# RWKV products in unbroken bursts over four quadrants, an output bank opened by its first product, and adaLN weights loaded at high priority

## The chip, the core and the metric

The kernel runs on one core of a Trainium2 chip, with its five engines: TensorE (PE in the profile; its weight loads are PEld), VectorE (DVE), ScalarE (ACT), GpSimd (POOL) and SyncE (SP), which here issues most DMAs. The metric is the device time of one execution in microseconds.

## What is computed

Two layers of a hybrid backbone over 512 latent and 256 context tokens of width 1024. Layer 0 mixes with a bidirectional RWKV-7 (12 heads of 64) and a pooling mixer, then a SwiGLU FFN; layer 1 is a neighbourhood attention and an FFN. Every sub-layer is modulated by adaLN vectors: `mod = silu(c) @ ada_w[i] + ada_b[i]`. The change lies in the RWKV recurrence and in the adaLN products:

```python
def wkv_scan(S0, r, w, k, v, kk, b, reverse):
    def step(S, inp):
        r_t, w_t, k_t, v_t, kk_t, b_t = inp
        sa = -jnp.einsum('bhij,bhj->bhi', S, kk_t)
        S = S * w_t[:, :, None, :] + sa[..., :, None] * b_t[:, :, None, :] + v_t[..., :, None] * k_t[:, :, None, :]
        return S, jnp.einsum('bhij,bhj->bhi', S, r_t)
    ...
for d in range(2):
    S_c, yc = wkv_scan(S0, ...context..., rev)
    _, yl = wkv_scan(S_c, ...latents..., rev)
```

## The kernel before

**GEMMs.** Activations lie transposed, features on partitions. Each f32 GEMM is made of three f32r products of split operands (hi x hi, lo x hi, hi x lo): lines L123 to L125, in `mm3`. Their banks are named g (layer 0's input projections), s (the context's output projection and FFN, 256 columns) and y or w (the latents, 512 columns). `mm3` keeps its last product in `self.last`.

**RWKV.** The recurrence is worked out in chunks of 64 tokens. A `Job` takes two head pairs (`pair`, `pair + 1`; l in the code), both directions (d), and four chunks; there are nine, three for the context and six for the latents. In each, the two heads (h) of a pair lie on partitions 0 to 63 and 64 to 127 (`hd[h]`). A job has
- `prep`: `scores` (L1157, 16 products of 64 x 64 by 128 columns for each l and d, so 36 groups of 16) and `tokens` transposes, for both l and d; then `inverse`, the inverse of a triangular 64 x 64 matrix for each chunk, whose 16 x 16 diagonal blocks DVE works out (L1191, L1192; the blocks go to it through HBM, tensors ar, L, td) and whose larger blocks TensorE joins in the steps s1 to s5;
- `chain`: four steps, one after the other. A step makes g (L1285), the first part of the output y (L1293, in a bank that two zero products of L1291 opened, since several products add up in it), copies the state into the next one's bank (L1298), then pa (L1302), the new rows of ST (ACT copies for head 0, DVE for head 1), the new state pS (L1315), which DVE scales into the next ST, and the last part of y (L1328).

The array of TensorE is 128 x 128. A product with 64 rows and 64 columns takes a quadrant of it. In what follows A and D are the two on the diagonal (rows and columns 0 to 63, rows and columns 64 to 127), B and C the other two (B: rows 0 to 63, columns 64 to 127). An f32 product appears in the profile as two records.

**Order.** The code gives each instruction a priority: `level(n)` sets the class (0 is served first) and within it the order of writing counts. A list scheduler with a timeline of its own then writes each engine's queue; an engine works its queue off in order. `issue_after(x)` forces an instruction behind x on the queue of the same engine, and lets others stand between. `emit` deals out several generators by their costs: in the latents' RWKV part a job's `chain` is level 0, the next job's `prep` level 2, and the context's output projection and FFN (s) level 8, which fills TensorE.

**adaLN.** `adas` multiplies silu(c) with `ada_w`: eight products of 32 output columns for a group of 512 features, in two bursts of four, one for each column strip (L201), then four small ones (L213) that turn the result. The weights come by `ada_loads` (SP, L180). In layer 0's mix groups 4 to 11 run at level 5, and their loads land in the three `wraw` buffers that the input weights `w_in` (L115) use too. Layer 1's twelve groups run at level 9, dealt out beside the latents' first FFN, with four buffers `aw` of their own.

## Time and profile before

| | |
|---|---|
| median of 3 runs (lowest, highest) | 2385.91 us (2370.8, 2388.42) |
| the profiled execution | 2381.51 us, its span 2379.5 us |
| busy: PE, PEld | 2163.1 us (91%), 1735.9 us (73%) |
| busy: DVE, ACT, POOL | 1226.7 us (52%), 994.5 us (42%), 660.5 us (28%) |
| granted TensorE clock, mean | 0.937 of 2.4 GHz |

Busy times are unions of an engine's instructions; a TensorE that is busy need not be at its peak. Up to about 690 us the input projections and the context's RWKV run, up to about 1015 us the latents' RWKV with the context's GEMMs as filler; then the context's rest and the latents' output projection and FFN, and from about 1620 us layer 1.

### The profile page before, as it was taken

To read this page: it belongs to the slowest core of one execution; us is meant where nothing else is said; L and a number is where in the kernel's file an instruction comes from. 1 tells how busy PE (TensorE), PEld (TensorE's weight loads), DVE (VectorE), ACT (ScalarE), POOL (GpSimd) and SP (SyncE) were. 2 spreads that over 40 slices of the span, in tenths; PEclk is the share of its full clock that TensorE was granted. 3 is DMA by queue.
4 is the path that set the end of the run, shared out by engine and by line. 5 is a ranking of instruction groups with operands and counts; after the bars stand their busy time and mean duration, and the time that the engine had idled before them with its cause. 6 is when DMAs were issued, how large, how long until landed. Compare 5 with 4: busy or idle time off the path is not lost.

```text
span 2379.5 us, 44426 instructions
## 1 busy us (share of the span) xinstructions
PE 2163.1 (91%) x16944; PEld 1735.9 (73%) x16944; DVE 1226.7 (52%) x2529; ACT 994.5 (42%) x2075; POOL 660.5 (28%) x643
## 2 busy tenths in 40 slices
PE   6787988889879898979999999998999998999995
PEld 4676666556657777757788887787878876888874
DVE  2666555636746764244534453347556665333343
ACT  3545344444534544334443342224455644322332
POOL 2442213121322433456642310005224442000021
PEclk9889999879879899999999999999999998999997
DMA  7766476666753544576544335332432112333331
GB/s 262 224 187 188 121 205 186 175 176 187 228 142 89 137 128 112 169 233 214 162 150 118 116 120 167 113 91 88 133 105 63 51 63 66 97 92 100 96 90 63
DMA packets 324677, 327.34 MB, mean 138 GB/s; under 512 B 137328, under 2 KB 214768, under 8 KB 324464
## 3 DMA queue, kind: packets, MB, share of 16 engines
q1 hardware_dynamic: 320720, 317.45, 45.1%
q10 hardware_dynamic: 2592, 3.90, 0.5%
q8 instruction: 133, 2.18, 0.4%
q0 software_dynamic: 1152, 3.15, 0.3%
q14 instruction: 80, 0.66, 0.1%
HBM read 280.02 MB, written 42.80 MB: 136 GB/s over the span
## 4 chain that ended last, share of the span: by engine, by line
PE 62%; DVE 6%; DMA 5%; issue 2%; ACT 2%; SPq 1%; POOL 1%; POOLq 0%; ACTq 0%; DVEq 0%
PE y L123 7%; PE y L125 7%; PE y L124 7%; PE w L123 6%; PE w L124 6%; PE w L125 6%; PE s L123 3%; PE s L125 3%; PE s L124 3%; PE s L743 1%; PE w L1157 1%; DMA wraw<-w 1%; PE v L201 1%; PE v L725 1%; PE y L700 1%
## 5 line engine op out<-in xcount | busy, mean ns | idle before, releaser
L887 ACT CAST whi<-wraw 128x512 fp32r<-128x512 f32 (+2 forms) x560 | 330.2, 594 | 674.1 <-PE y L124 261.0
L888 DVE TENSOR_TENSOR wlo<-wraw,whi 128x512 fp32r<-128x512 f32 (+2 forms) x384 | 293.1, 767 | 339.6 <-ACT whi L887 316.1
L888 POOL TENSOR_TENSOR wlo<-wraw,whi 128x512 fp32r<-128x512 f32 (+2 forms) x176 | 202.3, 1155 | 299.4 <-ACT whi L887 270.7
L123 PE MATMUL w<-lhhi,whi 128*128 128x512 f32 x472 | 189.3, 403 | 11.3 <-ACT lhhi L1012 5.8
L110 POOL TENSOR_TENSOR wlo<-wraw,whi 128x512 fp32r<-128x512 f32 x92 | 121.4, 1323 | 280.1 <-ACT whi L109 233.3
L123 PE MATMUL y<-lhhi,whi 128*128 128x512 f32 x488 | 192.3, 394 | 0.5 <-ACT lhhi L752 0.5
L124 PE MATMUL y<-lhlo,whi 128*128 128x512 f32 x488 | 190.7, 391 | 0.0
L125 PE MATMUL y<-lhhi,wlo 128*128 128x512 f32 x488 | 190.6, 391 | 0.0
L124 PE MATMUL w<-lhlo,whi 128*128 128x512 f32 x472 | 186.4, 395 | 1.3 <-DVE lhlo L937 1.1
L125 PE MATMUL w<-lhhi,wlo 128*128 128x512 f32 x472 | 185.6, 393 | 0.1
L913 POOL TENSOR_TENSOR lxz<-lxz,s 128x512 f32<-128x512 f32 x28 | 43.3, 1578 | 508.9 <-ACT s L919 508.9
L123 PE MATMUL s<-chhi,whi 128*128 128x256 f32 x480 | 145.5, 303 | 19.6 <-DVE kclo L616 7.8
L123 PE MATMUL g<-hhi,whi 128*128 128x256 f32 (+1 forms) x368 | 139.1, 378 | 17.4 <-DVE nr L486 4.5
L125 PE MATMUL s<-chhi,wlo 128*128 128x256 f32 x480 | 143.2, 298 | 1.1 <-POOL wlo L888 1.1
L124 PE MATMUL s<-chlo,whi 128*128 128x256 f32 x480 | 143.3, 299 | 0.4 <-DVE chlo L937 0.4
L125 PE MATMUL g<-hhi,wlo 128*128 128x256 f32 (+1 forms) x368 | 135.6, 369 | 2.2 <-POOL wlo L110 2.1
L124 PE MATMUL g<-hlo,whi 128*128 128x256 f32 (+1 forms) x368 | 132.6, 360 | 0.0
L123 PEld LDWEIGHTS s<-chhi,whi 128*128 128x128 f32 x480 | 97.2, 203 | 29.9 <-ACT whi L887 8.8
L123 PEld LDWEIGHTS w<-lhhi,whi 128*128 128x128 f32 x472 | 89.2, 190 | 36.0 <-ACT lhhi L984 7.4
L123 PEld LDWEIGHTS y<-lhhi,whi 128*128 128x128 f32 x488 | 92.1, 189 | 22.1 <-issue 3.0
L124 PEld LDWEIGHTS w<-lhlo,whi 128*128 128x128 f32 x472 | 89.3, 189 | 23.6 <-DVE lhlo L937 4.2
L125 PEld LDWEIGHTS y<-lhhi,wlo 128*128 128x128 f32 x488 | 91.9, 188 | 19.8 <-DVE n L937 0.8
(376 smaller groups left out, 5048.3 us busy)
## 6 DMA issues: line engine op xcount, KB each, us to landing
wraw<-w SPq DMA_DIRECT2D x368, 256.0 KB, 2.6
aw<-ada_w SPq DMA_DIRECT2D x128, 256.0 KB, 4.7
wraw<-w_in SPq DMA_DIRECT2D x92, 256.0 KB, 3.3
bk<-bk SPq DMA_DIRECT2D x72, 256.0 KB, 4.3
wraw<-ada_w SPq DMA_DIRECT2D x64, 256.0 KB, 3.4
wraw<-w_out SPq DMA_DIRECT2D x48, 256.0 KB, 3.0
wraw<-wk SPq DMA_DIRECT2D x32, 256.0 KB, 2.9
wraw<-wv SPq DMA_DIRECT2D x32, 256.0 KB, 3.1
```

Of the source, the lines that this page charges most:

```text
L110: (self.nc.gpsimd if POOL_LO else self.nc.vector).tensor_tensor(out=lo, in0=raw, in1=hi, op=ALU.subtract)
L123: mm(ps, lhsT=lh, rhs=rh, start=first, stop=False)
L124: mm(ps, lhsT=lh, rhs=rl, start=False, stop=False)
L125: self.last = mm(ps, lhsT=ll, rhs=rh, start=False, stop=last)
L201: mm = nc.tensor.matmul(ps[32 * q:32 * q + 32, part], lhsT=self.cs[:, k + q, :], rhs=w[q // step][:, q % step, :], start=k == 0, stop=k > ...
L700: return lambda: mm(banks[j][:, 256 * c:256 * c + 256], lhsT=q[i == 2][hd, cb * P:cb * P + P], rhs=r[i == 1][hd, cs], start=i == 0, stop=i ...
L725: turn = lambda j, i: lambda: nc.tensor.transpose(out=pt[j][:, i, :], in_=s[j][:, i * P:i * P + P], identity=self.ident)
L743: return lambda: mm(po[64 * j:64 * j + 64, :], lhsT=src[:, hc], rhs=sT[j][:, i, :], start=i == 0, stop=i == 3)
L887: self.nc.scalar.copy(out=hi, in_=raw)
L888: self.lo.tensor_tensor(out=lo, in0=raw, in1=hi, op=ALU.subtract)
L913: tt = lambda o, x, y, op, e=V: e.tensor_tensor(out=o, in0=x, in1=y, op=op)
L1157: nc.tensor.matmul(ps[w][hd[h ^ w], c, :], lhsT=bk[hd[h], w, c, :], rhs=LH[0][hd[h], c, :], start=True, stop=True,)
```

## The change

- `burst(calls)` is new: each product is issued after the one ahead of it.
- Scores: one burst of 16 that goes c outside, then w = 1, 0, then h, where w was outside. By quadrants: B C A D, four times, where it was A D four times and then B C four times.
- s1 to s5 and all products of a chain step become bursts, with head 1 ahead of head 0. pS goes by turns between the heads; before it did the four of head 0 and then the four of head 1.
- The zero products (L1291) go. The output bank is opened by the first product of each head (`start=l == d == 0`).
- `ada_loads` issues its DMAs at level 0, whatever the level of the products.
- The four adaLN products of a burst are issued after each other, the first of them after `self.last`, the last GEMM product written so far.

```diff
@@ ada_loads, adas
-                    self.nc.sync.dma_start(out=wv, in_=src[:, k:k + step, part])
+                    with self.level(0):
+                        self.nc.sync.dma_start(out=wv, in_=src[:, k:k + step, part])
...
-                    first = None
-                    for q in (3, 2, 1, 0):
-                        with self.tc.issue_after(first.ins) if first else nullcontext():
-                            mm = nc.tensor.matmul(
...
-                        first = first or mm
+                    with self.tc.issue_after(self.last.ins) if self.last else nullcontext():
+                        self.burst([lambda q=q: nc.tensor.matmul(
+                            ps[32 * q:32 * q + 32, part], lhsT=self.cs[:, k + q, :], rhs=w[q // step][:, q % step, :],
+                            start=k == 0, stop=k > 0, tile_position=(0, 32 * q)) for q in (3, 2, 1, 0)])
@@ burst
+    def burst(self, calls):
+        last = None
+        for c in calls:
+            with self.tc.issue_after(last.ins) if last else nullcontext():
+                last = c()
@@ scores
-        for w in range(2):
-            for c in range(4):
-                for h in range(2):
-                    nc.tensor.matmul(
-                        ps[w][hd[h ^ w], c, :], lhsT=bk[hd[h], w, c, :], rhs=LH[0][hd[h], c, :],
-                        start=True, stop=True,
-                    )
+        K.burst([
+            lambda w=w, c=c, h=h: nc.tensor.matmul(
+                ps[w][hd[h ^ w], c, :], lhsT=bk[hd[h], w, c, :], rhs=LH[0][hd[h], c, :], start=True, stop=True,
+            ) for c in range(4) for w in (1, 0) for h in range(2)
+        ])
@@ inverse, and so s2 to s5
-        uh = [(u, h) for u in range(8) for h in range(2)]
+        uh = [(u, h) for u in range(8) for h in (1, 0)]
-            for u, h in uh:
-                mm(px[hd[h], u, :], lhsT=A1[g][hd[h], u, :], rhs=Tm[g][hd[h], u, :], start=True, stop=True)
+            K.burst([lambda u=u, h=h: mm(
+                px[hd[h], u, :], lhsT=A1[g][hd[h], u, :], rhs=Tm[g][hd[h], u, :], start=True, stop=True) for u, h in uh])
@@ chain, and so pg, pa and the last py
-        ldh = [(l, d, h) for l in range(2) for d in range(2) for h in range(2)]
+        ldh = [(l, d, h) for l in range(2) for d in range(2) for h in (1, 0)]
-            for h in range(2):
-                mm(flat(py[hd[h]]), lhsT=K.zero[hd[h], 0:64], rhs=K.zero[hd[h], 0:256], start=True, stop=False)
-            for l, d, h in ldh:
-                mm(py[hd[h], d, l, :], lhsT=LH[l][d][h][:, ci[d], 64:128], rhs=ST[h][:, l, si, d, :], start=False, stop=False)
+            K.burst([lambda l=l, d=d, h=h: mm(
+                py[hd[h], d, l, :], lhsT=LH[l][d][h][:, ci[d], 64:128], rhs=ST[h][:, l, si, d, :],
+                start=l == d == 0, stop=False) for l, d, h in ldh])
...
-                for h in range(2):
-                    m0 = None
-                    for l in range(2):
-                        for d in range(2):
-                            with K.tc.issue_after(m0.ins) if m0 else nullcontext():
-                                m0 = mm(pS[hd[h], l, d, :], lhsT=TOK[l][d][:, h, ci[d], :], rhs=ST[h][:, l, si, d, :],
-                                        start=s == 0, stop=s == 0 or l == d == 1)
+                K.burst([lambda l=l, d=d, h=h: mm(
+                    pS[hd[h], l, d, :], lhsT=TOK[l][d][:, h, ci[d], :], rhs=ST[h][:, l, si, d, :],
+                    start=s == 0, stop=s == 0 or l == d == 1) for l, d, h in ldh])
```

Since the scheduler sees other instructions and constraints, all queues are written anew. At three places TensorE's queue reads as follows (tile names carry their buffer numbers).

The first score group of the first job, before: w_1338 is the bank of w = 0 (quadrants A and D), w_1339 that of w = 1 (B and C); L424 and L456 are products of `keys`, L496 a transpose.

```order
L424 MATMUL k_1040<-lora_511,lw_953 128x256
L496 MATMUL g_924<-cst_63,sq_808 128x128 x2
L1157 MATMUL w_1338<-lh_1331,bk_1328 64x128 x8
L1157 MATMUL w_1339<-lh_1331,bk_1328 64x128 x8
L456 MATMUL k_1132<-lora_552,lw_953 128x256
L123 MATMUL g_949<-hhi_427,whi_939 128x256
```

The same group after the change:

```order
L421 MATMUL k_1040<-lora_511,lw_953 128x256
L493 MATMUL g_924<-cst_63,sq_808 128x128 x2
L1160 MATMUL w_1339<-lh_1331,bk_1328 64x128 x2
L1160 MATMUL w_1338<-lh_1331,bk_1328 64x128 x2
L1160 MATMUL w_1339<-lh_1331,bk_1328 64x128 x2
L1160 MATMUL w_1338<-lh_1331,bk_1328 64x128 x2
L1160 MATMUL w_1339<-lh_1331,bk_1328 64x128 x2
L1160 MATMUL w_1338<-lh_1331,bk_1328 64x128 x2
L1160 MATMUL w_1339<-lh_1331,bk_1328 64x128 x2
L1160 MATMUL w_1338<-lh_1331,bk_1328 64x128 x2
L453 MATMUL k_1132<-lora_552,lw_953 128x256
L123 MATMUL g_949<-hhi_427,whi_939 128x256
```

The two banks now take turns, two products each; nothing else is changed around them.

The first chain step of the last job, before (c is the bank of g, S of the state, y of the output; L1298 copies the state):

```order
L1285 MATMUL c_13834<-ST_13027,lh_13279 64x64
L1285 MATMUL c_13834<-ST_13028,lh_13280 64x64
L1298 MATMUL S_13856<-ST_13027,cst_63 64x256
L1298 MATMUL S_13856<-ST_13028,cst_63 64x256
L1291 LDWEIGHTS zero_67
L1291 MATMUL y_13845<-zero_67 64x256
L1291 LDWEIGHTS zero_67
L1291 MATMUL y_13845<-zero_67 64x256
L1293 MATMUL y_13845<-ST_13027,lh_13087 64x64
L1293 MATMUL y_13845<-ST_13028,lh_13088 64x64
L1293 MATMUL y_13845<-ST_13027,lh_13135 64x64
```

The same step after the change:

```order
L1287 MATMUL c_13770<-ST_12969,lh_13151 64x64
L1287 MATMUL c_13770<-ST_12970,lh_13222 64x64
L1287 MATMUL c_13770<-ST_12969,lh_13221 64x64
L1293 MATMUL y_13781<-ST_12970,lh_13030 64x64
L1293 MATMUL y_13781<-ST_12969,lh_13029 64x64
L1293 MATMUL y_13781<-ST_12970,lh_13078 64x64
L1293 MATMUL y_13781<-ST_12969,lh_13077 64x64
L1293 MATMUL y_13781<-ST_12970,lh_13152 64x64
```

The zero products with their weight loads are gone, the heads have changed places (ST_12970 is head 1), and the output's first burst follows that of g at once; the state's copy (L1300) comes behind it. In one other step of this job GEMM products of the context stand between the two bursts.

The adaLN products of layer 1's second group, before, in the RWKV chain of the last job (v is their bank):

```order
L125 MATMUL s_6938<-chhi_6885,wlo_8165 128x256
L123 MATMUL s_6938<-chhi_6885,whi_8182 128x256
L124 MATMUL s_6938<-chlo_6886,whi_8182 128x256
L201 MATMUL v_14894<-aw_14883,cs_69 32x512
L1315 MATMUL S_13968<-ST_13027,tok_13122 64x64
L1315 MATMUL S_13968<-ST_13027,tok_13168 64x64
```

The first burst of layer 1's first group, after the change:

```order
L125 MATMUL s_6914<-g_8945,wlo_9139 128x256
L124 MATMUL w_14627<-lhlo_14131,whi_14630 128x512
L125 MATMUL w_14627<-lhhi_14130,wlo_14631 128x512
L200 MATMUL v_14646<-aw_14644,cs_69 32x512
L200 MATMUL v_14646<-aw_14642,cs_69 32x512
L200 MATMUL v_14646<-aw_14640,cs_69 32x512
L200 MATMUL v_14646<-aw_14638,cs_69 32x512
L124 MATMUL y_14628<-lhlo_14131,whi_14687 128x512
L125 MATMUL y_14628<-lhhi_14130,wlo_14688 128x512
```

It has moved from the last RWKV jobs to the latents' FFN (y, w, 512 columns): of layer 1's 96 products 48 stood ahead of the context's 1200th GEMM product, and now none does. On SP the loads of `w_in` and `ada_w` into the three `wraw` buffers keep their sequence among each other; ada loads stand up to some eight places further ahead among the other DMAs.

## Rows read from the trace of the kernel before

**Rows 1.** Windows of three stages: busy us (and count) by engine; granted clock, DMA share, GB/s.
```profile
0.00:690.00 690.00, 572.09 (x5751) 428.54 (x5751) 398.12 (x988) 305.99 (x725) 177.74 (x169) 0.89 0.66 193
690.00:1015.00 325.00, 296.27 (x4202) 247.70 (x4203) 174.61 (x475) 145.68 (x337) 118.72 (x122) 0.89 0.47 126
...
1110.00:1620.00 510.00, 506.91 (x2617) 417.87 (x2616) 233.35 (x356) 188.70 (x343) 133.35 (x118) 1.00 0.41 127
```

**Rows 2.** The chain that ended last, by line, in 525:690, 690:1015 and 1015:1110 us.
```profile
by line: PE g L123 6.6%; PE g L125 5.7%; PE g L124 5.5%; PE w L1157 5.4%; DMA kk<-kk 4.8%; issue 4.0%; DMA wraw<-w_out 3.5%; DMA mt<-mix 3.5%; DMA wraw<-ada_w 2.6%; PE g L565 2.4%; SPq L870 2.4%; DMA gate<-gate 2.4%; DMA kk<-k 2.4%; DMA bk<
...
by line: PE s L123 7.7%; PE s L124 6.8%; PE s L125 6.8%; PE w L1157 6.0%; DVE pr L1191 5.6%; PE S L1315 4.1%; issue 3.7%; PE c L1302 3.7%; PE c L1285 3.3%; DMA wraw<-w 3.3%; PE y L1328 3.1%; DMA ar<-AR 2.8%; DMA L<-ar 2.7%; PE y L1293 2.7%;
...
by line: DMA wraw<-w 13.3%; PE s L123 9.4%; PE s L125 9.1%; PE s L124 8.0%; PE v L201 8.0%; DMA lxz<-xp 6.0%; POOL wlo L888 5.9%; DMA aw<-ada_w 5.4%; POOL lxz L871 3.3%; PE w L124 3.2%; issue 3.0%; PE w L125 2.9%; PE w L123 2.9%; DVE Y L136
```

**Rows 3.** Groups of PE in 690:1015 (two) and in 525:690 us (one).
```profile
L1157 PE MATMUL w<-lh,bk 64*64 64x128 f32 x384 | 27.7, 304 | 0.7 <-PE y L1328 0.6
L1315 PE MATMUL S<-ST,tok 128*64 128x64 f32 x272 | 19.8, 233 | 0.7 <-DVE ST L1305 0.7
...
L1157 PE MATMUL w<-lh,bk 64*64 64x128 f32 x256 | 18.0, 285 | 0.9 <-DVE lh L1109 0.9
```

**Rows 4.** Timeline of PE: start, duration (us), line, operation, records; three places.
```profile
532.05 1.09 PE L1157 MATMUL w<-lh,bk 64*64 64x128 f32 x16
533.07 0.97 PE L1315 MATMUL S<-ST,tok 128*64 128x64 f32 x16
...
756.60 1.59 PE L1157 MATMUL w<-lh,bk 64*64 64x128 f32 x32 [0.65 <-PE y L1328]
758.12 0.87 PE L1285 MATMUL c<-ST,lh 128*64 128x64 f32 x16
...
902.22 0.63 PE L1302 MATMUL c<-g,TT 64*64 64x64 f32 x16
902.68 1.32 PE L1157 MATMUL w<-lh,bk 64*64 64x128 f32 x28
```

**Rows 5.** Timeline of PE in 975:981 us, a chain step between GEMMs.
```profile
975.41 0.28 PE L123 MATMUL s<-chhi,whi 128*128 128x256 f32 x1
975.53 0.28 PE L124 MATMUL s<-chlo,whi 128*128 128x256 f32 x1
975.74 0.97 PE L1315 MATMUL S<-ST,tok 128*64 128x64 f32 x16
976.63 0.68 PE L1328 MATMUL y<-ST,RB 64*64 64x64 f32 x16
...
979.62 0.69 PE L1285 MATMUL c<-ST,lh 128*64 128x64 f32 x16
980.23 0.30 PE L1291 MATMUL y<-zero 64*64 64x256 bf16 x2
980.46 0.69 PE L1293 MATMUL y<-ST,lh 128*64 128x64 f32 x16
```

**Rows 6.** Groups of PE over the whole span: busy, mean ns, idle before, releasers.
```profile
L1157 PE MATMUL w<-lh,bk 64*64 64x128 f32 x1152 | 81.0, 303 | 11.8 <-DVE lh L1109 10.4 <-ACT tok L1141 0.7 <-PE y L1328 0.6
...
L1315 PE MATMUL S<-ST,tok 128*64 128x64 f32 x528 | 39.7, 235 | 2.6 <-ACT ST L1304 1.9 <-DVE ST L1305 0.7
```

**Rows 7.** Waits of PE and of SP's DMA queue: total us, times, longest.
```profile
PE g L201 <- DMA wraw<-ada_w: 20.1, 11, 3.4
...
SPq L180 <- PE g L201: 17.5, 13, 4.7
```

**Rows 8.** Groups of PE in 960:1110 us: the adaLN products of layer 1.
```profile
L201 PE MATMUL v<-aw,cs 128*32 128x512 f32 x96 | 18.3, 710 | 2.5 <-DMA aw<-ada_w 2.5
...
L213 PE MATMUL v<-cst,md 128*128 128x2 f32 x40 | 4.9, 241 | 0.7 <-ACT md L210 0.7
```

**Rows 9.** Windows of the two long stretches at half clock.
```profile
460.00:494.00 34.00, 24.79 (x140) 14.66 (x142) 18.35 (x64) 12.60 (x34) 0.00 (x0) 0.50 0.70 194
679.00:706.00 27.00, 19.05 (x208) 15.61 (x209) 16.39 (x41) 10.91 (x25) 11.52 (x13) 0.50 0.55 133
```

More of the change, by code (lines that the diff above doesn't have):

```diff
@@ L77, in __init__ @@
         self.now = 0
-        self.tail = None
+        self.tail = self.last = None
         self.ps = {}
@@ L196, in adas @@
                     w = [ready.pop(0) for _ in range(count)]
-                    first = None
-                    for q in (3, 2, 1, 0):
-                        with self.tc.issue_after(first.ins) if first else nullcontext():
-                            mm = nc.tensor.matmul(
-                                ps[32 * q:32 * q + 32, part], lhsT=self.cs[:, k + q, :], rhs=w[q // step][:, q % step, :],
-                                start=k == 0, stop=k > 0, tile_position=(0, 32 * q),
-                            )
-                        first = first or mm
+                    with self.tc.issue_after(self.last.ins) if self.last else nullcontext():
+                        self.burst([lambda q=q: nc.tensor.matmul(
+                            ps[32 * q:32 * q + 32, part], lhsT=self.cs[:, k + q, :], rhs=w[q // step][:, q % step, :],
+                            start=k == 0, stop=k > 0, tile_position=(0, 32 * q)) for q in (3, 2, 1, 0)])
                     if k == 0 or part.stop < 512:
@@ L1242, in s2 @@
             p1 = K.bank(self.v, (8, 32))
-            for u, h in uh:
-                mm(p1[lo[h], u, :], lhsT=TT[g][lo[h], u, 0:32], rhs=X1[g][lo[h], u, 0:32], start=True, stop=True,
-                   tile_position=(64 * h, 64 * h))
+            K.burst([lambda u=u, h=h: mm(
+                p1[lo[h], u, :], lhsT=TT[g][lo[h], u, 0:32], rhs=X1[g][lo[h], u, 0:32], start=True, stop=True,
+                tile_position=(64 * h, 64 * h)) for u, h in uh])
             for h in range(2):
@@ L1249, in s3 @@
             p2 = K.bank(self.v, (8, 64))
-            for u, h in uh:
-                mm(p2[hd[h], u, :], lhsT=X1[g][hd[h], u, :], rhs=TT[g][hd[h], u, :], start=True, stop=True)
+            K.burst([lambda u=u, h=h: mm(
+                p2[hd[h], u, :], lhsT=X1[g][hd[h], u, :], rhs=TT[g][hd[h], u, :], start=True, stop=True) for u, h in uh])
             V.tensor_tensor(out=TT[g], in0=TT[g], in1=p2, op=ALU.subtract)
@@ L1255, in s4 @@
             p3 = K.bank(self.v, (8, 32))
-            for u, h in uh:
-                mm(p3[up[h], u, :], lhsT=A1[g][lo[h], u, 32:64], rhs=Tm[g][lo[h], u, 0:32], start=True, stop=True,
-                   tile_position=(64 * h, 64 * h + 32))
+            K.burst([lambda u=u, h=h: mm(
+                p3[up[h], u, :], lhsT=A1[g][lo[h], u, 32:64], rhs=Tm[g][lo[h], u, 0:32], start=True, stop=True,
+                tile_position=(64 * h, 64 * h + 32)) for u, h in uh])
             for h in range(2):
@@ L1262, in s5 @@
             p4 = K.bank(self.v, (8, 32))
-            for u, h in uh:
-                mm(p4[lo[h], u, :], lhsT=Tm[g][up[h], u, 0:32], rhs=TT[g][up[h], u, 32:64], start=True, stop=True,
-                   tile_position=(64 * h + 32, 64 * h))
+            K.burst([lambda u=u, h=h: mm(
+                p4[lo[h], u, :], lhsT=Tm[g][up[h], u, 0:32], rhs=TT[g][up[h], u, 32:64], start=True, stop=True,
+                tile_position=(64 * h + 32, 64 * h)) for u, h in uh])
             for h in range(2):
@@ L1283, in chain @@
             pg = small()
-            for l, d, h in ldh:
-                mm(pg[hd[h], l, d, :], lhsT=LH[l][d][h][:, ci[d], 0:64], rhs=ST[h][:, l, si, d, :], start=True, stop=True)
+            K.burst([lambda l=l, d=d, h=h: mm(
+                pg[hd[h], l, d, :], lhsT=LH[l][d][h][:, ci[d], 0:64], rhs=ST[h][:, l, si, d, :], start=True, stop=True) for l, d, h in ldh])
             g = K.rp.tile([P, 2, 2, 64], F32, name="g", tag="g", bufs=2)
@@ L1289, in chain @@
             py = K.bank("y", (2, 2, 64))
-            for h in range(2):
-                mm(flat(py[hd[h]]), lhsT=K.zero[hd[h], 0:64], rhs=K.zero[hd[h], 0:256], start=True, stop=False)
-            for l, d, h in ldh:
-                mm(py[hd[h], d, l, :], lhsT=LH[l][d][h][:, ci[d], 64:128], rhs=ST[h][:, l, si, d, :], start=False, stop=False)
+            K.burst([lambda l=l, d=d, h=h: mm(
+                py[hd[h], d, l, :], lhsT=LH[l][d][h][:, ci[d], 64:128], rhs=ST[h][:, l, si, d, :],
+                start=l == d == 0, stop=False) for l, d, h in ldh])
             if 0 < s < NC - 1:
@@ L1300, in chain @@
             pa = small()
-            for l, d, h in ldh:
-                mm(pa[hd[h], l, d, :], lhsT=TT[l][hd[h], 4 * d + ci[d], :], rhs=g[hd[h], l, d, :], start=True, stop=True)
+            K.burst([lambda l=l, d=d, h=h: mm(
+                pa[hd[h], l, d, :], lhsT=TT[l][hd[h], 4 * d + ci[d], :], rhs=g[hd[h], l, d, :], start=True, stop=True) for l, d, h in ldh])
             nc.scalar.copy(out=ST[0][hd[0], :, si], in_=pa[hd[0]])
@@ L1326, in chain @@
                     )
-            for l, d, h in ldh:
-                mm(py[hd[h], d, l, :], lhsT=RB[l][hd[h], 4 * d + ci[d], :], rhs=ST[h][hd[h], l, si, d, :],
-                   start=False, stop=l == d == 1)
+            K.burst([lambda l=l, d=d, h=h: mm(
+                py[hd[h], d, l, :], lhsT=RB[l][hd[h], 4 * d + ci[d], :], rhs=ST[h][hd[h], l, si, d, :],
+                start=False, stop=l == d == 1) for l, d, h in ldh])
             for d in range(2):
```

2 lines of the change are left out of this document (1 added, 1 removed).

## The prediction

> **What bounds the kernel now.** I read the stages first [rows 1]: TensorE is the bound from 1110 us on (506.91 of 510 us busy at full clock), and there the diff changes almost nothing. The RWKV part, 0 to 1015 us, is where the edits lie, and it is only nearly bound by TensorE: 572.09 of 690 and 296.27 of 325 us busy, at a granted clock of 0.89, that is, with some 22% of the time at 1.2 instead of 2.4 GHz. Next the chain that ended last [rows 2]: besides the GEMMs (g, s) it holds the small RWKV products (scores L1157, state L1315, L1302, L1285, L1328), but also DVE's inverse (L1191) and trips through HBM (ar, L, kk). So a microsecond taken from TensorE there is worth less than one. How much less: in 690 to 1015 us L1157 and L1315 are 6.0% and 4.1% of 325 us on the chain, 19.5 and 13.3 us, of 27.7 and 19.8 us busy [rows 2, 3], 69%; in 525 to 690 us L1157 is 5.4% of 165, 8.9 of 18.0 us, 49%. For the time before 525 us, where no chain was read, I take 49% too.
>
> **Scores in four quadrants.** A score group is 16 products, in records 32 (an f32 product runs in two passes). Before, eight use the two quadrants on the diagonal and then eight the other two. Half a group, 16 records, starts at 532.05 and the next line at 533.07 [rows 4]: 1.02 us. From this goes a change of array shape: the 16 records of L1302 take 0.46 us up to a line of the same shape, and those of L1285 take 0.61 up to another shape [rows 4, 5], so a switch costs 0.15 us. A half is then 0.87 us for eight steps of 0.109. That four quadrants do run side by side is shown by the seam: a whole group takes 1.52 us (756.60 to 758.12) and not 2.04 less a switch, 1.89; the second half starts 0.37 us before the first is through. Now order the products B C A D: eight steps in all, 0.87 us. Counted in the orders of the two programs: before, 14 of 36 groups stand unbroken, so 36 x 1.74 - 14 x 0.37 = 57.5 us; after, all 36 take 0.87, and 17 have two products cut off ahead of the other 14, which costs two steps (0.22) each: 35.0 us. Saved **22.4 us** at full clock.
>
> Weighed against this: the Trainium skill, "TensorE: Matmul & The Clock Gate", Part 3, "What overlaps and what doesn't", says that a weight load runs beside matmuls in flight only when its row group differs. A and B share rows, C and D too; by that rule the new order would save nothing here. The seam of 0.37 us in the trace speaks against it.
>
> **State products by turns.** L1315 ran four products of one head and then four of the other, all in one half of the columns each. Unbroken (20 of 33 times) 0.89 us to the next start (975.74 to 976.63 [rows 5]), less a switch 0.74; in two pieces (13 times) 2 x 0.46. By turns they need 0.46 like L1302, which already alternates. Saved 20 x 0.28 + 13 x 0.46 = **11.6 us**. The first product now waits for DVE's copy of ST[1] instead of ACT's of ST[0]; the last one waited for it before too and had 0.46 us of work behind it, as now, so I price the wait at nothing; at worst 33 x 0.28 = 9 us. Queued behind it on TensorE stand L1328 and the GEMMs, and DVE's next state waits for it.
>
> **No zero products.** A pair takes 0.23 us to the next start (980.23 to 980.46 [rows 5]), 0.08 less the switch: 36 x 0.08 = **3 us**. Its wait for the y bank passes to L1293's first product, 16 of which now wait for ACT where the zero product did: the same buffers and readers, so I price it at nothing.
>
> **Whole bursts.** Changes of shape with an RWKV product on a side fall from 648 to 498 in the two orders (64 of the 150 are those of the zero products): 150 x 0.15 = **22.5 us**. By the 0.09 us that only the entry costs (975.53 to 975.74 is 0.21 us where the GEMM's step is 0.12 [rows 5]) it would be 13.5.
>
> **Sum on TensorE**: 22.4 + 11.6 + 3 + 22.5 = 59.5 us at full clock, at the stage's clock 59.5 / 0.89 = **67 us**. As a check, 57.5 us and 64 switches of 0.15 at that clock are 75 us against the 81.0 us of L1157's row [rows 6]. Of 59.5 some 26 belong to 690 to 1015 us: 34% of the scores (27.7 of 81.0) and half of the rest (19.8 of 39.7 for L1315) [rows 3, 6]. So 26.2 / 0.89 x 0.69 = 20 us, and 33.3 / 0.89 x 0.49 = 18 us: **39 us** of the 67 reach the end. What is late next is DVE's inverse and its DMAs, which stay.
>
> **Early adaLN weights.** TensorE waited 20.1 us for them, 11 times, at most 3.4 us [rows 7]. But in the layer 0 mix they land in the same three buffers as the input weights, which SP fills in the same sequence before and after, and SP itself waited 17.5 us for TensorE to give a buffer back [rows 7]. A load that can't start earlier gains nothing: I take 0. Ends: 20 us gained; 10 lost, if an ada load holds a buffer early and the w_in load behind it on SP lands late three times (3 x 3.4).
>
> **adaLN products behind the last GEMM.** In 960 to 1110 us 48 of layer 1's products (96 records, 18.3 us, and 4.9 of L213 [rows 8]) ran as filler. Now each burst comes after the GEMM last written, which is the latents' FFN, so all 48 go past 1110 us, where TensorE has no room; 60 more products of the context, 0.12 us each, come forward in exchange (7 us). Up to 23 - 7 = 16 us lost; but in 1015 to 1110 us L201 and its aw loads were 8.0 + 5.4% of 95 us on the chain, 13 us, which go [rows 2]. I take 0, ends -13 and +16.
>
> **Forecast.** 2379.5 us is the profile's span, 2381.5 the profiled execution; less 39 it is 2342.5. The median of the three runs, 2385.91, lies 4.4 us above the profiled execution, so I forecast **2347 us**, 1.6% faster. A measurement of this kernel can tell about 1% from no change, 24 us: 2362 and 2410.
>
> **Rivals.**
> First, TensorE is the bound after all: idle there [rows 1] is 118 and 29 us in the two stages, the rest GEMMs that could use every freed slot. Then all 67 us reach the end: 2319. Against it speaks the chain, half of which isn't TensorE in 525 to 690 us. Chance 0.15.
> Second, the RWKV part is bound by its latency: each freed slot turns into a wait for DVE, ACT or HBM, since bursts issue as wholes and nothing fills the hole inside. If a quarter of the 67 us gets through, 17 us: 2369, no change that can be told. For it: L1191 and the ar, L and kk transfers on the chain. Against it: L1157 there itself. Chance 0.2.
> Third, one row group is one lane: the scores save nothing, 25 of the 67 us go. Left are 18.6 / 0.89 x 0.69 + 18.5 / 0.89 x 0.49 = 25 us: 2361, at the edge of what can be told. Chance 0.05, counted within 1%. The rule of the Trainium skill named above would have it so.
> Fourth, slower, by TensorE's clock. Twice the clock fell to 0.50 for long, at 460 and at 679 us, and TensorE was then busy for 24.79 of 34 and 19.05 of 27 us with small products and waits among them [rows 9]. Shorter bursts between the same waits leave TensorE idle for longer. At 1.2 GHz each microsecond loses half of one. To be 1% slower the clock must eat the 39 us and 24 more, 126 us more at 1.2 GHz beside some 223 now; that is, it decides when the granted clock of 0 to 1015 us falls from 0.89 under 0.83 (349 of 1015 us at 1.2 GHz): 2410 and more. Chance 0.08.
>
> **How the numbers follow.** The forecast (a half to two thirds of the saving, 2330 to 2361) has the remaining 0.52. Faster by over 1%: 0.52 + 0.15 = 0.67. Within 1%: 0.2 + 0.05. Slower: 0.08. The range runs from the first rival with part of the adaLN gain, 2312, to the second with some of the 16 us of moved products, 2384; beyond lie the fourth and the ends of the others, 0.15 or so.
>
> **What would show it.** L1157's row (a new line number) should fall from 81.0 to about 50 us busy, L1315's from 39.7 to about 25; no zero row; the last RWKV step some 35 us earlier than now and the later stages as long as now; the wait for ada_w still near 20 us. Wrong would be: score bursts that still take 1.5 us (the third rival), rows that shrink while waits on DVE and DMA grow (the second), a granted clock well under 0.89 (the fourth), or a later FFN stage that takes over 10 us longer (the moved products).

## The result and the profile after

The change makes the kernel **slower by 1.1%**: 2407.11 us (median of 4 runs, 2402.39 to 2411.4) beside 2383.94 us (4 runs), a ratio of 1.0106 with a 95% interval of 1.0061 to 1.0151. The forecast was 2347 us, faster. One execution of one kernel below, the profiled one of scores_only, took 3820 us beside 2403 to 2418 in its five others; it is left out, and its trace isn't read.

The windows of the kernel after, in the stages of [rows 1], with the same columns:

```profile
0.00:690.00 690.00, 545.22 (x5414) 403.94 (x5414) 381.02 (x960) 298.40 (x708) 166.12 (x157) 0.84 0.63 186
690.00:1015.00 325.00, 268.34 (x4278) 231.84 (x4280) 182.20 (x485) 148.57 (x346) 123.86 (x133) 0.85 0.47 128
...
1110.00:1620.00 510.00, 505.26 (x2629) 403.89 (x2628) 222.51 (x348) 182.22 (x329) 127.82 (x114) 1.00 0.48 147
```

In the last of these stages TensorE is as busy as it was. In the first two it is busy for 27 and 28 us less, but it isn't done sooner: at 690 us 337 fewer of its records are through (at most 72 of them zero products). The time went into waits, and the granted clock fell from 0.89 to 0.84 and 0.85, that is, more of the time at 1.2 GHz. Over the whole kernel, the sums of all windows (before, then after):

```profile
sum 2500.00, PE 2163.14 PEld 1735.86 DVE 1226.71 ACT 994.49 POOL 660.54; mean PE 721.05 PEld 578.62 DVE 408.90 ACT 331.50 POOL 220.18
```

```profile
sum 2500.00, PE 2125.32 PEld 1703.12 DVE 1218.92 ACT 992.29 POOL 657.77; mean PE 708.44 PEld 567.71 DVE 406.31 ACT 330.76 POOL 219.26
```

TensorE is busy for 37.8 us less. Its idle time, the span less the busy time, grew from 2379.5 - 2163.1 = 216.4 to 2400.5 - 2125.3 = 275.2 us, by 58.8. The difference is the 21 us by which the span grew.

The groups of PE over the whole span, after (columns as in [rows 6]): scores, the tokens transposes, pS; then the transposes of before:

```profile
L1160 PE MATMUL w<-lh,bk 64*64 64x128 f32 x1152 | 62.1, 300 | 12.5 <-DVE lh L1113 5.4 <-DMA wraw<-w 3.4 <-DVE RB L1152 2.0
...
L1178 PE MATMUL w<-cst,bk 128*128 128x128 f32 x144 | 26.0, 306 | 24.7 <-DVE lh L1152 24.2 <-DVE modT L214 0.3
L1312 PE MATMUL S<-ST,tok 128*64 128x64 f32 x528 | 25.4, 246 | 7.7 <-DVE ST L1307 7.7
```

```profile
L1175 PE MATMUL w<-cst,bk 128*128 128x128 f32 x144 | 24.8, 296 | 4.5 <-DVE RB L1148 2.2 <-DVE lh L1148 1.6 <-DVE q L426 0.6
```

Scores fell from 81.0 to 62.1 us, pS from 39.7 to 25.4 [rows 6]. The largest new wait is that of the transposes: 24.2 us for DVE to empty a bank w. One of its places, TensorE's timeline after and then DVE's:

```profile
110.60 1.46 PE L1160 MATMUL w<-lh,bk 64*64 64x128 f32 x32 [2.40 <-DVE lh L1113]
117.45 1.08 PE L1178 MATMUL w<-cst,bk 128*128 128x128 f32 x4 [5.39 <-DVE lh L1152]
```

```profile
113.78 0.41 DVE L1113 TENSOR_TENSOR lh<-r,Pt 128x256 f32<-128x256 f32 x1
...
115.45 0.42 DVE L1152 TENSOR_TENSOR A<-w,cst 128x256 f32<-128x256 f32 x1
115.91 1.39 DVE L1152 TENSOR_TENSOR lh<-w,cst 64x512 f32<-64x512 f32 x2
```

Both banks of the scores are full at the same moment, 112 us; DVE, which has other work first, empties one at 117.3, and the transposes, which need a bank w, stand at the head of TensorE's queue for 5.39 us.

The last part of y of the last chain step starts 14 us later (before, then after: duration, first and last start):

```profile
L1328 PE MATMUL y<-ST,RB x576: 218/218/366, 192.6 to 1013.4; 64*64 64x64 f32 x192
```

```profile
L1325 PE MATMUL y<-ST,RB x576: 216/218/366, 195.0 to 1027.2; 64*64 64x64 f32 x192
```

So of the 21 us of span 14 are lost by the end of the RWKV part and 7 behind it. Most of it is lost early: the last of the input projections (g, hi x hi) starts 18 us later (before, then after):

```profile
L123 PE MATMUL g<-hhi,whi x368: 276/392/797, 39.0 to 658.2; 128*128 128x256 f32 x92, 128*128 128x512 f32 x92
```

```profile
L123 PE MATMUL g<-hhi,whi x368: 276/393/797, 35.3 to 676.4; 128*128 128x256 f32 x92, 128*128 128x512 f32 x92
```

The chain that ended last, by line, in 690 to 1015 us, after (before: [rows 2]):

```profile
by line: PE s L123 5.9%; issue 5.3%; PE s L124 5.2%; PE s L125 4.9%; PE v L1253 4.2%; PE w L1160 4.0%; DVE pr L1194 3.4%; DMA wraw<-w 3.3%; SPq L1230 3.2%; DMA mt<-mix 3.1%; DMA Pt<-pt 2.7%; DMA L<-ar 2.7%; DMA TT<-td 2.5%; DVE Y L1362 2.5%
```

With all lines of an engine added up, TensorE's part of this chain fell from 60 to 43% of the stretch, while transfers rose from 13 to 19%, DVE from 16 to 20% and SP's queue from 5 to 8%. The small products are fewer in it, as forecast, but other work took their place, and the end came no nearer.

### The profile page after: what moved, and what is told of

Its sections match the earlier page's. It is cut to its first block, busy times and chain, and to the rows that moved or that the text cites. A ratio compares the mean times of both kernels' runs of the same rounds, so it can differ in the third digit from the quotient of the medians.

```text
span 2400.5 us, 44348 instructions
## 1 busy us (share of the span) xinstructions
PE 2125.3 (89%) x16872; PEld 1703.1 (71%) x16872; DVE 1218.9 (51%) x2529; ACT 992.3 (41%) x2075; POOL 657.8 (27%) x643
## 4 chain that ended last, share of the span: by engine, by line
PE 66%; DMA 13%; DVE 10%; SPq 3%; issue 3%; ACT 3%; POOL 1%; POOLq 0%; ACTq 0%; DVEq 0%
PE y L123 7%; PE y L125 7%; PE y L124 7%; PE w L123 6%; PE w L124 6%; PE w L125 6%; PE s L123 3%; PE s L124 2%; PE s L125 2%; DMA Pt<-pt 2%; PE g L123 2%; PE g L125 1%; DMA wraw<-w_in 1%; PE g L124 1%; DVE pr L1194 1%
## 5 line engine op out<-in xcount | busy, mean ns | idle before, releaser
L123 PE MATMUL g<-hhi,whi 128*128 128x256 f32 (+1 forms) x368 | 144.4, 393 | 20.8 <-ACT whi L109 5.5
L123 PEld LDWEIGHTS g<-hhi,whi 128*128 128x128 f32 x368 | 79.2, 215 | 42.2 <-issue 17.6
L124 PEld LDWEIGHTS y<-lhlo,whi 128*128 128x128 f32 x488 | 91.7, 188 | 22.3 <-issue 3.8
```

The costliest lines, as they stand in the source:

```text
L123: mm(ps, lhsT=lh, rhs=rh, start=first, stop=False)
L124: mm(ps, lhsT=lh, rhs=rl, start=False, stop=False)
```

## The experiments

Every kernel was timed beside the kernel before, in 4 to 12 executions. Busy and idle time are TensorE's (idle is span less busy), the clock is its mean over the span, and the last column is the last start of the y part above. These three come from one execution each, and executions of one kernel lie up to 28 us apart, so a difference of a few us there means nothing by itself. "Rest" is the change without the score burst and the adaLN edits.

| kernel | ratio to before, 95% interval | busy, idle us | clock | RWKV end us |
|---|---|---|---|---|
| before | 1 | 2163.1, 216.4 | 0.937 | 1013.4 |
| the change | 1.0106 (1.0061 to 1.0151) | 2125.3, 275.2 | 0.919 | 1027.2 |
| no_ada: rest + scores | 0.9984 (0.9959 to 1.001) | 2116.2, 256.8 | 0.930 | 1013.5 |
| ada_only | 1.0067 (1.0045 to 1.0089) | 2168.8, 231.1 | 0.929 | 1013.3 |
| old_scores: rest + adaLN | 0.9962 (0.994 to 0.9984) | 2119.5, 257.6 | 0.935 | 1003.1 |
| scores_only | 1.0111 (1.0073 to 1.0149) | not read | | |
| rest_only | 1.0042 (1.0021 to 1.0063) | 2130.4, 259.3 | 0.922 | 1018.5 |
| ada_and_scores | 1.0131 (1.0106 to 1.0156) | 2157.8, 249.0 | 0.928 | 1038.8 |
| burst_w_outer | 1.0058 (1.0035 to 1.0081) | 2128.0, 262.8 | 0.924 | 1014.5 |
| tokens_first | 0.9991 (0.9971 to 1.0011) | 2118.9, 251.2 | 0.922 | 1013.1 |
| ada_after_gemm | 1.0162 (1.0132 to 1.0191) | 2173.5, 243.2 | 0.926 | 1030.0 |
| heads_swapped | 1.0147 (1.0119 to 1.0175) | 2153.4, 260.8 | 0.923 | 1037.5 |
| u_reversed | 0.9991 (0.9975 to 1.0008) | 2157.9, 220.6 | 0.939 | 1009.5 |
| head0_first | 1.0188 (1.0162 to 1.0214) | 2175.5, 250.5 | 0.906 | 1038.7 |
| head0_no_ada | 1.0102 (1.0072 to 1.0132) | 2158.9, 236.1 | 0.927 | 1029.7 |
| head0_old_scores | 1.0157 (1.0131 to 1.0182) | 2161.0, 247.5 | 0.926 | 1027.7 |
| all_tokens_first | 1.01 (1.0074 to 1.0125) | 2125.8, 274.9 | 0.921 | 1032.8 |
| tokens_first_old_scores | 1.0029 (1.0014 to 1.0044) | 2126.2, 260.2 | 0.927 | 1008.7 |
| all_by_rows | 1.0265 (1.0235 to 1.0295) | 2258.1, 200.4 | 0.916 | 1100.6 |
| no_blocks | 0.9839 (0.9813 to 0.9866) | 2110.5, 233.8 | 0.931 | 943.7 |

The expectations name these theories. 1: the score burst fills both w banks at once and holds up the transposes. 2: the adaLN edits cost the time (2a the products behind the GEMM, 2b the early loads). 3: the bursts of the inverse and the chain do. A: the parts' effects add up. B: whatever TensorE saves turns into waits. C: each edit makes the scheduler rewrite the queues, and the luck of the new order decides. D: the new order of the heads has a price of its own.

**Which part costs it?** Four kernels leave out or hold one part.

no_ada, the change with the adaLN lines of before:

```diff
-                    with self.level(0):
-                        self.nc.sync.dma_start(out=wv, in_=src[:, k:k + step, part])
+                    self.nc.sync.dma_start(out=wv, in_=src[:, k:k + step, part])
...
-                    with self.tc.issue_after(self.last.ins) if self.last else nullcontext():
-                        self.burst([lambda q=q: nc.tensor.matmul(
...
+                    for q in (3, 2, 1, 0):
+                        with self.tc.issue_after(first.ins) if first else nullcontext():
+                            mm = nc.tensor.matmul(
...
```

> All edits of the change but the two on adaLN: loads and products stay as before. Theory 1 (the score burst fills both w banks and holds up the tokens transposes): still slower than before by 10 to 20 us, the waits of the tokens transposes near 24 us. Theory 2 (adaLN products tied behind a GEMM cost the time, in the first part and behind the latents' first FFN): most of the 24 us come back, at most 5 us slower than before, attention no later than 1750 us. Theory 3 (whole bursts in the inverse and the chain open holes on TensorE): slower by 15 to 25 us as the whole change.

ada_only, the kernel before with these adaLN lines of the change (the diff the other way round).

> The kernel before with the two adaLN edits alone. Theory 1 and theory 3: within 5 us of before. Theory 2: slower by 10 to 20 us, with some 10 us of it between the first latent GEMM and attention.

old_scores, the change with the scores of before:

```diff
-        K.burst([
-            lambda w=w, c=c, h=h: nc.tensor.matmul(
...
-            ) for c in range(4) for w in (1, 0) for h in range(2)
...
+        for w in range(2):
+            for c in range(4):
+                for h in range(2):
+                    nc.tensor.matmul(
...
```

> The whole change but for the scores, which keep their order of before (A D four times, then B C four times, no burst). Theory 1: 15 to 25 us faster than the whole change, that is level with before, and the waits of the tokens transposes back under 10 us. Theory 2 and theory 3: as slow as the whole change or slower still, since 19 us of TensorE's saving go with the score burst.

scores_only, the kernel before with the score burst (this diff the other way round).

> The kernel before with the score burst alone. Theory 1: slower than before by 8 to 20 us, tokens waits over 15 us. Theory 2 and theory 3: faster than before by 5 to 15 us, since TensorE's 19 us of saving stand against nothing.

Measured: each part alone is slower (1.0067, 1.0111), and the change without either is not slower than before. That suits theory 1 and theory 2 together, and theory 3 falls: the bursts of the inverse and the chain are in the two fastest. If the effects added up, the rest alone had to be over 1% faster. Two runs complete the eight combinations.

rest_only, the change with both diffs above undone; ada_and_scores, the kernel before with both done.

> Bursts of the inverse and the chain, pS by turns and no zero products, without the score burst and without the adaLN edits. Theory A (effects add up): no_ada less scores_only and old_scores less ada_only give 1.1 to 1.3% faster than before, 25 to 30 us. Theory B (TensorE's freed time turns into waits whatever is done, the two edits left out only shift it): no more than 0.4% faster, as old_scores.

> The kernel before with the adaLN edits and the score burst, the eighth of the eight combinations. Theory A, by the sums of single effects (0.67 and 1.11%): 1.6 to 2.0% slower than before. Theory C: anywhere from 0.5% faster to 2% slower, no sum of the two.

rest_only is 0.42% **slower**, so theory A falls. From the eight combinations, the step in percent that each part makes, in the four surroundings (the other two parts absent, one of them there, both there):

| part | neither | one | the other | both |
|---|---|---|---|---|
| adaLN | +0.67 | +0.20 (scores) | -0.80 (rest) | +1.22 |
| scores | +1.11 | +0.64 (adaLN) | -0.58 (rest) | +1.44 |
| rest | +0.42 | -1.05 (adaLN) | -1.27 (scores) | -0.25 |

The step of each part changes its sign with what stands beside it, and its two ends lie further apart than the intervals. No part has one price. Theory B, by which the saving turns into waits, fits: rest_only is busy for 33 us less and idle for 43 us more than before.

**The wait that the score burst adds.** burst_w_outer is rest_only with a score burst that keeps w outside, tokens_first is no_ada with the transposes written first, all_tokens_first the same in the whole change, tokens_first_old_scores the same in old_scores.

```diff
@@ burst_w_outer
-            ) for c in range(4) for w in (1, 0) for h in range(2)
+            ) for w in range(2) for c in range(4) for h in range(2)
@@ tokens_first, all_tokens_first, tokens_first_old_scores
-                self.scores(l, d, bk)
                 self.tokens(l, d, bk)
+                self.scores(l, d, bk)
```

> rest_only and a score burst of 16 that keeps w outside (A D four times, then B C four times). Theory 1 (bank): the bank of w = 0 is done half a burst early again, so from the last score product to the first tokens transpose it takes near 3.1 us as in before and old_scores, and the time is within 5 us of rest_only. Rival (that no other product may stand inside a burst of 16 is what costs): as slow as no_ada, 15 to 25 us slower than rest_only.

> no_ada (four-quadrant score burst, no adaLN edits), with the tokens transposes written ahead of the scores of the same l and d, so that they don't wait for the scores' banks. Theory 1: the waits of the tokens transposes (15.8 us in no_ada) go under 5 us, and the time comes to that of rest_only or up to 10 us under it: 10 to 30 us faster than no_ada. Rival (the score burst costs by itself, by TensorE's clock or its filler): as no_ada, within 5 us.

> The whole change, with the tokens transposes written ahead of the scores. Theory 1 (their waits for a w bank, 24.2 us in the whole change, are what costs): 15 to 25 us faster than the whole change, level with before. Theory C (a wait taken away turns up elsewhere, and the order decides): TensorE's idle time changes by less than half of the 24 us, and the time lies anywhere from 10 us faster to 20 us slower than before.

> old_scores with the tokens transposes written ahead of the scores. It is the order that might beat both kernels: if old_scores' 0.4% and tokens_first's 0.1% over no_ada add up, 0.4 to 0.6% faster than before. Theory C: no sum, between 0.5% faster and 1.5% slower.

burst_w_outer is level with rest_only: that a burst is whole doesn't cost by itself. As a mean over the 36 groups of each timeline, 2.9 us pass from the start of the last score product to that of the first transpose in before, 2.9 in burst_w_outer, and 4.9 in no_ada and in the change. So the wait does come from both banks being done at once. But taking it away gains nothing: tokens_first is level with no_ada, and all_tokens_first has the same span as the change, 2400.7 and 2400.5 us (22 us slower than before, where theory 1 had it level and theory C allowed 20). Where the wait went is seen in two groups, all_tokens_first first, the change behind it (its transposes are shown above):

```profile
L123 PE MATMUL g<-hhi,whi 128*128 128x256 f32 (+1 forms) x368 | 144.9, 394 | 35.3 <-ACT whi L109 14.2 <-DVE k L263 9.7 <-DVE k L494 5.4
...
L1178 PE MATMUL w<-cst,bk 128*128 128x128 f32 x144 | 27.1, 317 | 10.1 <-issue 7.8 <-PE k L421 0.9 <-ACT z L1375 0.7
```

```profile
L123 PE MATMUL g<-hhi,whi 128*128 128x256 f32 (+1 forms) x368 | 144.4, 393 | 20.8 <-ACT whi L109 5.5 <-DVE k L263 4.4 <-DVE nr L483 4.1
```

The transposes wait 14.6 us less, the input projections g 14.5 us more, and the idle time is 274.9 and 275.2 us. Theory 1 falls: the wait is real, but TensorE loses the same time elsewhere when it is gone. With the old scores the transposes first made it slower (1.0029 beside 0.9962).

**The adaLN edits apart.** ada_after_gemm is the kernel before with the second edit alone, the loads at their old level.

> The kernel before with one of the adaLN edits: bursts of four behind the GEMM product last written, loads at their old level. Theory 2a (the 48 products pushed behind the last GEMM cost it): as ada_only, 0.5 to 0.9% slower than before, attention near 1760 us. Theory 2b (the early loads cost it, by taking weight buffers): within 5 us of before.

It is slower than both edits together (1.0162 and 1.0067, more than theory 2a had), so theory 2b falls: the early loads don't cost, and in this surrounding they give 0.95% back. Behind the RWKV part (span less RWKV end) ada_only takes 1386.6 us, before 1366.1, ada_after_gemm 1386.7; the change 1373.3, no_ada 1359.5; old_scores 1374.0, rest_only 1371.2. So here the edit costs 20.5, 20.6 and 13.8 us in three pairs. The 2.8 us of the fourth show nothing: u_reversed takes 2.9 us more than before here and heads_swapped 10.6, without any adaLN edit. The groups of PE in 1110 to 1760 us show it (before, then after):

```profile
L201 PE MATMUL v<-aw,cs 128*32 128x512 f32 x96 | 14.9, 605 | 1.8 <-DMA aw<-ada_w 1.8
...
L213 PE MATMUL v<-cst,md 128*128 128x2 f32 x56 | 6.8, 236 | 0.0
```

```profile
L200 PE MATMUL v<-aw,cs 128*32 128x512 f32 x192 | 29.7, 605 | 0.0
...
L210 PE MATMUL v<-cst,md 128*128 128x2 f32 x96 | 11.8, 236 | 0.0
```

All 192 records now lie in the stage that TensorE bounds: 29.7 - 14.9 + 11.8 - 6.8 = 19.8 us more there. (In exchange, products of the context move ahead of 1110 us.) What changes the sign of the adaLN step is the first stage: with the adaLN edits the last input projection (g, hi x hi) starts later in two pairs, 672.2 us in ada_only beside 658.2 and 676.4 in the change beside 650.3 in no_ada, but earlier in a third, 656.4 in old_scores beside 679.1 in rest_only.

**Is the RWKV part bound by TensorE or by its latency?** all_by_rows makes TensorE's RWKV products dearer, no_blocks shortens the latency and leaves TensorE's products as they are (it leaves out part of the inverse).

```diff
@@ all_by_rows: no_ada, with
-            ) for c in range(4) for w in (1, 0) for h in range(2)
+            ) for h in range(2) for c in range(4) for w in (1, 0)
...
-        uh = [(u, h) for u in range(8) for h in (1, 0)]
+        uh = [(u, h) for h in (1, 0) for u in range(8)]
...
-        ldh = [(l, d, h) for l in range(2) for d in range(2) for h in (1, 0)]
+        ldh = [(l, d, h) for h in (1, 0) for l in range(2) for d in range(2)]
@@ no_blocks: no_ada, with
-        for b in range(4):
-            nc.sync.dma_start(out=rows(L, b), in_=diag(ar, b))
-        yield 2
-        for t in range(1, 8):
...
+        for cost in (2, *[0.4] * 7, 1.2, 1.2):
+            yield cost
```

> no_ada with the products inside each burst sorted so that all of one head come first (as pS was before): the same products in the same bursts, without heads side by side. By pS, which took 36.5 us in before and 22.2 in no_ada, a factor of 1.6, TensorE's RWKV products become some 120 us dearer. TensorE as the bound: 100 to 150 us slower than no_ada. Latency as the bound: the small products on the path get slower too, but most of it goes into the waits: 20 to 70 us slower.

> no_ada without the 16 x 16 diagonal blocks of the inverse on DVE (they are left out, X stays the identity) and without the loads of L from HBM: some 75 us of DVE and nine trips through HBM less, no product of TensorE less. Latency as the bound of the RWKV part: 30 to 100 us faster than no_ada. TensorE as the bound: less than 10 us faster.

The sums of all windows, no_ada, all_by_rows and no_blocks:

```profile
sum 2500.00, PE 2116.15 PEld 1702.05 DVE 1219.69 ACT 992.70 POOL 660.63; mean PE 705.38 PEld 567.35 DVE 406.56 ACT 330.90 POOL 220.21
```

```profile
sum 2500.00, PE 2258.08 PEld 1841.51 DVE 1218.95 ACT 993.49 POOL 658.48; mean PE 752.69 PEld 613.84 DVE 406.32 ACT 331.16 POOL 219.49
```

```profile
sum 2500.00, PE 2110.54 PEld 1696.46 DVE 1164.68 ACT 990.35 POOL 655.44; mean PE 703.51 PEld 565.49 DVE 388.23 ACT 330.12 POOL 218.48
```

142 us more of busy TensorE lengthened the profiled execution by 85 us, and 56 us came out of idle time; by the ratios (1.0265 less 0.9984, of 2381) it cost 67 us. 55 us less of DVE and nine trips through HBM less gave 34 us, with TensorE's busy time level. The 67 us lie at the upper end of what latency as the bound allowed, the 34 us at the lower. So both count: latency holds TensorE back, and TensorE is not free. In no_blocks the RWKV part ends 70 us earlier than in no_ada (943.7 and 1013.5), but the last product of the input projections starts no earlier:

```profile
L123 PE MATMUL g<-hhi,whi x368: 276/389/796, 39.3 to 649.1; 128*128 128x256 f32 x92, 128*128 128x512 f32 x92
```

```profile
L123 PE MATMUL g<-hhi,whi x368: 276/392/796, 36.5 to 650.3; 128*128 128x256 f32 x92, 128*128 128x512 f32 x92
```

(no_blocks, then no_ada.) So this part of the latency doesn't set the end of the input projections.

**Does the order alone move the time?** heads_swapped and u_reversed are the kernel before with the same instructions in another order.

```diff
@@ heads_swapped
-        uh = [(u, h) for u in range(8) for h in range(2)]
+        uh = [(u, h) for u in range(8) for h in (1, 0)]
...
-        ldh = [(l, d, h) for l in range(2) for d in range(2) for h in range(2)]
+        ldh = [(l, d, h) for l in range(2) for d in range(2) for h in (1, 0)]
@@ u_reversed
-        uh = [(u, h) for u in range(8) for h in range(2)]
+        uh = [(u, h) for u in range(7, -1, -1) for h in range(2)]
```

> The kernel before with nothing but the two heads' order in the products of the inverse and the chain turned round (head 1 first): the same instructions, the same work, another order of the queues. Theory C (every edit rewrites the queues, and what an edit costs or gives is mostly the luck of the new order): the time moves by 5 to 25 us, up or down. Theory A (parts have effects of their own): within 5 us of before.

> The kernel before with the eight blocks u of the inverse's products taken from 7 down to 0, the heads as before: the same instructions and work, and no product that any other engine feeds earlier or later by its place in a group, since every group waits for whole tiles. Theory C: the time moves by 5 to 25 us, up or down, with TensorE's waits. Theory D: within 5 us of before.

The order of the heads costs 1.47% with no work changed, 35 us, more than any theory had: 9.7 us less busy, 44 us more idle. The reversed blocks, though they reorder the queues too, cost nothing. So not every new order costs (theory C as put there is too wide), and the order of the heads, which is in the change, needed a test of its own: the change, no_ada and old_scores with head 0 first.

```diff
-        uh = [(u, h) for u in range(8) for h in (1, 0)]
+        uh = [(u, h) for u in range(8) for h in range(2)]
...
-        ldh = [(l, d, h) for l in range(2) for d in range(2) for h in (1, 0)]
+        ldh = [(l, d, h) for l in range(2) for d in range(2) for h in range(2)]
```

> The whole change, with head 0 ahead of head 1 again in the products of the inverse and the chain. Theory D (the new order of the heads costs by itself, since the state of head 1 comes last from DVE): 1.2 to 1.7% faster than the whole change, so 0.2 to 0.6% faster than before. Theory C (luck of the order): anywhere between 1% faster and 1.5% slower than before, no fixed step.

> no_ada with head 0 first again. Theory D: 1.2 to 1.7% faster than no_ada, so 1.4 to 1.9% faster than before. Theory C: no fixed step, between 1% faster and 1.5% slower than before.

> old_scores with head 0 first again. Theory D: 1.2 to 1.7% faster than old_scores, so 1.6 to 2.1% faster than before. Theory C: no fixed step, between 1% faster and 1.5% slower than before.

All three are slower than with head 1 first, by 0.8, 1.2 and 2.0%: theory D falls too, the step has the other sign (and two lie beyond theory C's 1.5%). Here the loss is on TensorE, which is busy for 50, 43 and 42 us more and idle for less. `issue_after` keeps the order in a burst but lets others stand between, and with head 0 first the first product goes as soon as head 0's state is there, and other work then fills the wait for head 1. Counted in the orders of the programs, the eight pS products stand in one piece 33 times of 33 in the change, 5 times in head0_first; the eight of the last y part 35 of 36 times, and 7. So it is the order of the heads that makes the bursts whole; that the broken bursts are what costs is read from these counts beside the busy time.

No kernel here that computes everything beats before by 1%; the fastest is old_scores, 0.38% faster.

## Why the prediction was wrong

**Right: the terms on TensorE.** A whole group of scores after (timeline of PE, columns as in [rows 4]):

```profile
299.54 1.10 PE L1160 MATMUL w<-lh,bk 64*64 64x128 f32 x32
300.57 0.69 PE L1312 MATMUL S<-ST,tok 128*64 128x64 f32 x16
301.18 0.51 PE L1325 MATMUL y<-ST,RB 64*64 64x64 f32 x10
```

From start to start a group takes 1.03 us, less a change of shape 0.88, where 0.87 was forecast; before took 1.52 unbroken, less the same 1.37, or 1.74 in two separate halves [rows 4]. pS takes 0.61, less 0.15 the forecast 0.46. So four quadrants do run side by side. The Trainium skill, "TensorE: Matmul & The Clock Gate", Part 3, "What overlaps and what doesn't", says that a weight load runs beside matmuls in flight only when its row group differs. By this rule, the third rival, the scores would save nothing; the 1.03 us beside 1.52 contradict it. The rows: pS 25.4 (25 forecast), no zero row, scores 62.1 (50 forecast). The forecast for the scores was too low, and not by the clock: a score record took 300 ns, 303 before. The same working had given 75 for the 81.0 of before, and in the queue after only 12 of the 36 groups stand in one piece, where the prediction broke 17, in one place each. Changes of shape number 648 and 498 in the traces too; what they cost by themselves isn't measured. The waits for the adaLN weights stayed at 21.4 us (20 forecast).

The sum holds as well. TensorE is busy at 1.2 GHz for 228.1 us before and 277.1 after; with these counted half, an estimate, its work at full clock is 2049.1 and 1986.8 us, 62.3 less, beside the 59.5 forecast. The 24.5 us between this and the 37.8 by which busy time fell went to the lower clock.

**Wrong: the step from TensorE to the end.** "39 us of the 67 reach the end" is the step that failed. The shares of the chain of waits, 69 and 49%, said which lines stood on the path that ended last; they were taken as the part of each freed microsecond that shortens it. In fact none did: in the change 58.8 us of new idle time and 24.5 us lost to the clock stand against the 62.3 us of saved work, and the last RWKV step starts 14 us later, not 35 earlier. With the rest of the change in, and its scores edit, a variant of it, its adaLN edits or neither (the five kernels no_ada, old_scores, rest_only, burst_w_outer, tokens_first), TensorE is busy for 33 to 47 us less and idle for 35 to 46 us more; by the ratios these kernels lie between 9 us faster and 14 us slower than before. By the chain after, transfers, DVE and SP's queue took the place of the small products; and a wait taken away in one place came back in another (all_tokens_first). In the other direction, in the one run that adds work, the share would have been about right: of 142 us added, 67 came through. Which new wait holds the end is not found.

**Wrong by rival.** The second rival, latency, let a quarter through; in fact nothing came through, and by its mechanism it is the nearest. Its reason, that nothing fills the hole inside a burst, is not so: `issue_after` lets others stand between, and they did. The fourth, the clock, was near by its number (2410) and was to decide from 0.83 down; 0.84 and 0.85 were granted, so some 95 us more of the 1015 at 1.2 GHz (twice 0.047 of them, 0.89 less 0.843). What this costs shows in products that the change doesn't touch, the 1104 of the input projections, 407.3 us busy before and 419.3 after, 3% more. One third of them took 139.1 and 144.4 us (378 and 393 ns each; of these 368, 55 and 75 began at 1.2 GHz, and the others took 353 and 351 ns):

```profile
L123 PE MATMUL g<-hhi,whi 128*128 128x256 f32 (+1 forms) x368 | 139.1, 378 | 17.4 <-DVE nr L486 4.5 <-DVE k L497 4.5 <-ACT whi L109 4.4
```

So rivals that were kept apart came together: more waits and more time at 1.2 GHz. That the waits bring the lower clock is not shown: old_scores is idle for 41 us more than before, at a clock of 0.935 beside 0.937.

**Wrong: three edits taken at 0.** The moved adaLN products have a price behind the RWKV part, 14 to 21 us in three pairs, at the upper end given (16) or a little beyond. The early loads gave 0.95%, 23 us, in the one pair that tells, where 20 was the upper end. The order of the heads had no term but a wait priced at nothing (at worst 9 us): with head 1 first 33 of 33 pS bursts are whole and with head 0 first 5, and in the kernel before the order alone costs 1.5%. And the parts were priced one by one and added up; the table of steps shows that here they don't add. A slip without weight: the forecast's own ends, 2330 and 2361, let 84 and 37% of the 67 us through, not two thirds and a half.

**Left open.** Why the same part gains in one surrounding and loses in another, and what sets the end of the input projections (649 to 706 us in these kernels), where most of the loss lies. A run in which TensorE's queue is the same, word for word, and only the products' own time differs would tell; the scheduler reorders with every such edit, so it wasn't tried. Nor was a fourth buffer for the input weights, the early loads alone, or the rest split further: pS by turns and the missing zero products have no run of their own.

## What to carry to other kernels

Here TensorE was busy for 83 and 91% of the two stretches and worked off one queue in order, and time freed on it was not time gained. In such a place price it at 0 until the wait that comes next is named, and try the largest new wait by taking it away before believing that it is the cause. Where a list scheduler writes the queues, time an edit that changes nothing but an order beside the real one (here 0.1 and 1.5%), and time parts in more than one surrounding. With `issue_after`, a burst stayed whole where its first product was the one that is ready last.

## What the runs showed of the hardware

Four 64 x 64 quadrants run f32 products side by side: 16 products in 0.88 us where two quadrants and then the other two took 1.37 unbroken. That TensorE's granted clock is 0.50 in stretches of small products with waits among them was known from [rows 9], at 73 and 71% busy; that a kernel whose TensorE is busy for 38 us less spends some 95 us more of its first 1015 at 1.2 GHz, and runs the untouched input projections 3% slower, was not expected.
